# First stretch of the mixers: TensorE in an order of emission that follows a rough account of its time, windows of the projection reordered

## The chip, the cores and the metric

The kernel runs on one core of one Trainium2 chip. The metric is the time of one execution on the device in microseconds (us); what is compared is the median over runs. Matrix products run on TensorE (PE in the profile), elementwise work on VectorE (DVE), ScalarE (ACT) and GpSimd (POOL), and transfers are issued by SyncE (SP), ScalarE and GpSimd.

## The reference

A trunk of two layers over 512 prompt positions and 8 samples of 4 positions, 544 columns in all. A layer is a gated feed-forward part, four mixers side by side, and a second feed-forward part:

```python
def _layer(x, pos0, st, p):
    x = x + 0.5 * _swiglu(_rmsnorm(x, p['norm_ffn1']), p['ffn1_in'], p['ffn1_out'])
    u = _rmsnorm(x, p['norm_mix']) @ p['w_in']
    u_ssd, u_rwkv, u_s5, u_pool = _split_at(u, (SSD_PROJ, RWKV_PROJ, GROUP_WIDTH, GROUP_WIDTH))
    ...
    y = jnp.concatenate([y_ssd, y_rwkv, y_s5, y_pool], axis=-1)
    x = x + y @ p['w_out']
    x = x + 0.5 * _swiglu(_rmsnorm(x, p['norm_ffn2']), p['ffn2_in'], p['ffn2_out'])
```

The mixers that matter here take slices of the projected `u` (the normalized input times `w_in`):

```python
# rwkv: shifted inputs, low-rank decay and rate, then a scan over time
xs = uf + (prev - uf) * mu
w_raw = -softplus(-(w0 + tanh(wd) @ w2)) - 0.5
a = sigmoid(a0 + ad @ a2);  g = sigmoid(gd) @ g2
kk = k * k_k;  kk = kk / max(sqrt(sum(kk * kk)), 1e-12)
# s5: a complex linear recurrence, gelu, then a gated product
y = gelu(real(C h) + u * d_skip)
ya, yb = split(y @ glu_w + glu_b);  out = ya * sigmoid(yb)
# pool: running means over 2, 4, 8 and 16 positions, minus u, times pool_w
```

All is float32; a large product is made of two-part operands, so that a block costs three products of TensorE's faster float32 type.

## The kernel before, in words

The 544 columns lie along the free dimension in two halves; features lie on the 128 partitions. A layer's **mixers** begin with the projection. Its output is cut into 21 *windows* of 128 features (the last one, `dt`, of 8), each named for what it carries: `wa` (decay and rate inputs of rwkv), `k0 k1 r0 r1 v0 v1 gd` (rwkv), `s0 s1` (S5), `p0 p1` (pooling), `B C x z dt` (the SSD mixer). A window is eight blocks of weights with six matmuls each (`mm3`, L839 to L841) into one of two large PSUM buffers (`psd`), and is then multiplied by the reciprocal norm on VectorE into a tile `u` (the eviction, L1047 and L1050). The table `WIN` gives the windows' order. `UB` = 3 tiles `u` go round.

The *first stretch*, from `wa` to the products KB,AB (L220), runs two flows: `s5` and, one behind the other, `rwkv_prep` and `pool`. They are Python generators, and `merge` (L101) picks the one with the smallest account; a `yield` adds a fixed cost to it. When a flow asks for a window with `U(n)`, `win()` emits windows until that one is there. What the program emits, a scheduler then places on each engine's queue; on TensorE it moves instructions of the stretch past each other where operands allow. A *second stretch* follows (the chunks of rwkv, its samples, the SSD mixer, the remaining windows).

The steps that the prediction speaks of, by name and line:

- `wa` is shifted (L146 to L149), its upper half goes through tanh on ScalarE (L152), and four products `xs,mat` (through the helper `mm544`, L126; each is two matmuls of 272 columns) give `sig` and `av` (L159, L160).
- `sq` (L167) and its product (`sq,cst`) give `ss` (L169); `rsqrt` (L132 to L135) and L173 to L187 then make the operands RA, KB and `xs` on VectorE.
- `s5` takes each half `t` of its groups through DRAM into `U8` (L710 to L713), multiplies by GT (L721), rotates and scans on VectorE (L725 to L733), rotates back into `HP` (L740), and multiplies by TP and CO (L749, L750). The result goes through DRAM into `yg` (L753), gets the skip term (L755) and gelu (L756). The products `yg,glu` (L764) need both halves.
- `pool` makes running sums by adds on VectorE (L563), forms `pP` (L574 to L579) and multiplies it.
- Weights are split into a rounded part `whi` on ScalarE (L823) and the rest `wlo` (L826), which in the mixers is GpSimd's.

Of the kernel before, what the change touches and what calls it, by code (L numbers as in the profile page):

```python
# [100 lines left out]
def merge(*flows):  # L101

    q=[[t,i,f,g] for i,(t,f,g) in enumerate(flows)]
    while q:
        e=min(q,key=lambda e:(e[0],e[1]))
        try: e[0]+=e[2]*next(e[3])
        except StopIteration: q.remove(e)
class Mix:
    def __init__(s,tc,nc,ctx):
        s.tc,s.nc,s.ctx=tc,nc,ctx  # L110
# [11 lines left out]
    def mm544(s,lhsT,rhs,fn):  # L122

        for i in range(2):
            ps=s.bank()[:,:H]; c=slice(i*H,(i+1)*H)
            s.nc.tensor.matmul(ps,lhsT,rhs[:,c],start=True,stop=True)  # L126
# [10 lines left out]
    def rwkv_prep(s,U,fp,tp,R):  # L137

        nc=s.nc; V=nc.vector; A=nc.scalar; G=nc.gpsimd; PE=nc.tensor
        tmp=lambda n="tmp": tp.tile([128,T],F32,name=n,tag="tmp")  # L140
        def shift(n,x=None):
# [7 lines left out]
            V.scalar_tensor_tensor(xv,us[:,:,1:5],om,ts,op0=OP.mult,op1=OP.add)  # L149
            return x  # L150
        wa=shift('wa')
        A.activation(wa[0:64],wa[0:64],AF.Tanh)  # L152
        yield 4
# [3 lines left out]
        for p in range(2):  # L157
# [6 lines left out]
            yield 4  # L164
            ra=fp.tile([128,2,T],F32,name=f"RA{p}"); kb=fp.tile([128,2,T],F32,name=f"KB{p}"); RA.append(ra); KB.append(kb)
            xk=shift(f'k{p}')
            sq=tmp("sq"); A.activation(sq,xk,AF.Square,scale=s.v('kk',p))  # L167
            ss=tmp("ss")
            s.mm544(s.c('j64'),sq,lambda ps,c: V.tensor_scalar(ss[:,c],ps,1e-24,None,op0=OP.max))  # L169
            A.activation(sig,sig,AF.Exp,scale=-DC); Ex=sig  # L170
            yield 4
# [6 lines left out]
            yield 4  # L178
# [5 lines left out]
            yield 4  # L184
# [155 lines left out]
    def rwkv_sample(s,R,S0,state_out,sp):  # L340
        nc=s.nc; V=nc.vector; A=nc.scalar; G=nc.gpsimd; PE=nc.tensor
# [216 lines left out]
    def pool(s,U,emit,tp):  # L558
# [5 lines left out]
        for t in range(2):  # L564
            u=U(t); F=tl("pF"); a=tl("pA")
# [5 lines left out]
            yield 5  # L571
# [7 lines left out]
            V.tensor_tensor(P[:,0:16],m,u[:,15:31],op=OP.subtract)  # L579
# [211 lines left out]
class Kern(Mix):  # L791
# [218 lines left out]
    def mixers(s,l,st):  # L1010
# [255 lines left out]
```

## Time and profile before

| | |
|---|---|
| median of 3 runs | 2235.03 us (2230.42 to 2238.39) |
| the profiled execution | 2238.23 us, its span 2236.1 us |
| TensorE busy | 2148.0 us (96% of the span) |
| VectorE, ScalarE, GpSimd busy | 69%, 53%, 25% |
| first stretch of layer 0 | 399.56 to 536.69 us |
| first stretch of layer 1 | 1500.82 to 1641.41 us |

The profile is one execution. A timeline row is one instruction, or a run of like ones with their count, with its start and length; behind it, in brackets, stands how long the engine was idle before it and what ended that. A matmul of float32 operands is two records. [...]

### The profile page before, as it was taken

Reading aid. Unit: us, or ns where it says so; the run is one execution under the profiler, and the core shown is the slowest. Engines: PE = TensorE matmul, PEld = TensorE weight load, DVE = VectorE, ACT = ScalarE, POOL = GpSimd, SP = SyncE. Lnnn points to the kernel's source line nnn. Section 1 sums busy time; section 2 is a strip of 40 time slices with the busy share of each in tenths; the row PEclk is TensorE's granted clock in tenths of the full one; section 3 lists DMA queues with packets and bytes.
Section 4 is the critical chain, followed back from the end, with each engine's and each line's share of the span. In section 5 each row is a group of like instructions: output and inputs, shape, how many; then the busy total and the mean of one; then the engine's idle time right before and its main releaser. Section 6 shows DMA issues by size and latency. Waiting matters only on the chain. (4 is left out here: it accounts for less than half of the span.)

```text
span 2236.1 us, 42540 instructions
## 1 busy us (share of the span) xinstructions
PE 2148.0 (96%) x16630; PEld 2091.5 (94%) x16630; DVE 1550.0 (69%) x2895; ACT 1195.2 (53%) x2251; POOL 555.4 (25%) x650
## 2 busy tenths in 40 slices
PE   8999999989999999999999999998889999999997
PEld 8999999987799989999999999998878999999997
DVE  7877775288866887777577666644887678666664
ACT  6755554365444675555465555535553446555542
POOL 2111121534313411112141111123432124111112
PEclk9999999999999999999999999999899999999999
DMA  6666564542213466656357565554332135665551
GB/s 183 177 146 173 150 157 143 199 122 97 80 38 127 116 165 152 164 150 162 108 120 180 133 144 154 132 164 151 111 100 71 44 128 131 155 151 147 134 140 46
DMA packets 151560, 298.62 MB, mean 134 GB/s; under 512 B 37184, under 2 KB 61888, under 8 KB 151360
## 3 DMA queue, kind: packets, MB, share of 16 engines
q1 hardware_dynamic: 101600, 187.51, 25.4%
q0 software_dynamic: 35712, 65.55, 17.7%
q10 hardware_dynamic: 14048, 42.85, 5.8%
q8 instruction: 130, 2.13, 0.4%
q14 instruction: 70, 0.57, 0.1%
HBM read 202.10 MB, written 28.22 MB: 103 GB/s over the span
## 5 line engine op out<-in xcount | busy, mean ns | idle before, releaser
L938 PE MATMUL pm<-AH,xh 128*128 128x272 f32 x2016 | 527.0, 290 | 12.7 <-DVE e L942 6.0
L938 PE MATMUL pm<-AL,xh 128*128 128x272 f32 x2016 | 525.6, 289 | 0.0
L823 ACT CAST whi<-wraw 128x512 fp32r<-128x512 f32 x356 | 218.9, 617 | 360.2 <-PE pd L840 300.7
L839 PE MATMUL pd<-xh,whi 128*128 128x272 f32 (+2 forms) x1408 | 388.3, 295 | 14.0 <-DVE u L1050 5.1
L938 PEld LDWEIGHTS pm<-AH,xh 128*128 128x128 f32 x2016 | 380.6, 189 | 15.2 <-DVE e L942 7.6
L840 PE MATMUL pd<-xl,whi 128*128 128x272 f32 (+2 forms) x1408 | 392.6, 294 | 1.2 <-DVE xl L857 1.2
L938 PEld LDWEIGHTS pm<-AL,xh 128*128 128x128 f32 x2016 | 380.4, 189 | 0.0
L839 PE MATMUL pd<-hh,whi 128*128 128x272 f32 x1396 | 376.6, 289 | 0.0
L840 PE MATMUL pd<-hl,whi 128*128 128x272 f32 x1396 | 376.0, 288 | 0.0
L939 PE MATMUL pm<-AH,xl 128*128 128x272 f32 x2016 | 337.3, 289 | 1.8 <-DMA xl<-wraw 1.8
L825 POOL DMA_DIRECT2D xl<-wraw x144 | 124.9, 868 | 800.1 <-DVE s L942 584.3
L841 PE MATMUL pd<-xh,wlo 128*128 128x272 f32 (+2 forms) x1408 | 301.0, 293 | 1.2 <-DVE wlo L826 0.9
L939 PEld LDWEIGHTS pm<-AH,xl 128*128 128x128 f32 x2016 | 287.4, 189 | 2.1 <-DMA xl<-wraw 2.1
L841 PE MATMUL pd<-hh,wlo 128*128 128x272 f32 x1396 | 287.3, 287 | 0.0
L839 PEld LDWEIGHTS pd<-xh,whi 128*128 128x128 f32 x1408 | 269.2, 191 | 19.3 <-issue 12.4
L840 PEld LDWEIGHTS pd<-xl,whi 128*128 128x128 f32 x1408 | 270.0, 192 | 4.8 <-DVE xl L857 1.8
L839 PEld LDWEIGHTS pd<-hh,whi 128*128 128x128 f32 x1396 | 262.7, 188 | 1.7 <-issue 1.7
L840 PEld LDWEIGHTS pd<-hl,whi 128*128 128x128 f32 x1396 | 262.3, 188 | 0.0
L841 PEld LDWEIGHTS pd<-xh,wlo 128*128 128x128 f32 x1408 | 228.5, 191 | 3.4 <-DVE wlo L826 2.3
L841 PEld LDWEIGHTS pd<-hh,wlo 128*128 128x128 f32 x1396 | 219.6, 188 | 0.0
L826 DVE TENSOR_TENSOR wlo<-wraw,whi 128x512 fp32r<-128x512 f32 x256 | 184.6, 721 | 43.7 <-ACT whi L823 37.6
L970 DVE SCALAR_TENSOR_TENSOR x<-pd,x 128x544 f32<-128x544 f32 x159 | 114.7, 721 | 97.6 <-PE pd L841 97.1
(510 smaller groups left out, 3604.2 us busy)
## 6 DMA issues: line engine op xcount, KB each, us to landing
wraw<-in_w SPq DMA_DIRECT2D x262, 512.0 KB, 4.0
xl<-wraw POOLq DMA_DIRECT2D x144, 256.0 KB, 3.9
wraw<-in_w ACTq DMA_DIRECT2D x59, 512.0 KB, 3.4
xl<-sqa POOLq DMA_DIRECT2D x72, 256.0 KB, 3.4
AL<-ss POOLq DMA_DIRECT2D x16, 272.0 KB, 5.4
AL<-sqa POOLq DMA_DIRECT2D x16, 272.0 KB, 4.4
xd<-x SPq DMA_DIRECT2D x16, 272.0 KB, 2.9
x<-xd SPq DMA_DIRECT2D x16, 272.0 KB, 4.7
```

Source lines behind the costliest of these rows:

```text
L823: nc.scalar.copy(hi,x)
L825: nc.scalar.mul(lo,x,-1.0); nc.gpsimd.dma_start(lo,x,accum_op=OP.add)
L826: else: s.lo.tensor_tensor(lo,x,hi.bitcast(F32),op=OP.subtract)
L839: nc.tensor.matmul(p,wh,rh[:,a:b],start=(n==0),stop=False)
L840: nc.tensor.matmul(p,wh,rl[:,a:b],start=False,stop=False)
L841: for p,a,b in o: nc.tensor.matmul(p,wl,rh[:,a:b],start=False,stop=(n==K-1))
L938: for t in F[j]: nc.tensor.matmul(o,wh[:,j,:],t[:,f,:],start=first and j==0 and t is F[j][0],stop=False,skip_group_check=True)
L939: for j in range(4): nc.tensor.matmul(o,wl[:,j,:],F[j][0][:,f,:],start=False,stop=j==3,skip_group_check=True)
L970: V.scalar_tensor_tensor(xv,po[:,:,:H],0.5,xv,op0=OP.mult,op1=OP.add)
```

## The change

A class `Queue` stands before TensorE in the mixers and the projection. It adds up a rough time `t` of what is issued, and while `on` (the first stretch) it binds every instruction of a step to the last TensorE instruction of the step before (`issue_after`), so that TensorE runs them in the order of emission. `drive` takes the place of `merge`: a flow goes on when the window it named has been evicted and the delay that it yielded has passed on that account; otherwise `fill` emits half a window (four blocks). `room` holds a window back while three tiles `u` live.

```diff
+class Queue:
...
+    def run(s,f,us):
+        s.t+=us
+        if s.on and s.gate is not None:
+            with s.tc.issue_after(s.gate): i=f()
+        else: i=f()
+        s.last=i.ins
+    def matmul(s,o,lhs,rhs,**k):
+        n=math.prod(rhs.shape[1:])
+        s.run(lambda: s.e.matmul(o,lhs,rhs,**k),n*0.00046 if lhs.dtype==F32R else max(0.2,n*0.00172))
...
+    def drive(s,flows,fill,at):
+        q=[[0.0,None,g] for g in flows]
+        def adv(f):
+            a=s.t; s.gate=s.last; r=f(); at['now']+=s.t-a
+            for n in s.new: at[n]=at['now']
+            s.new.clear()
+            return r
+        while q:
+            for e in q:
+                if e[1] in at: e[0]=at[e[1]]; e[1]=None
+            e=next((e for e in q if e[1] is None and e[0]<=at['now']),None)
+            if e is not None:
+                y=adv(lambda: next(e[2],None))
+                if y is None: q.remove(e)
+                elif isinstance(y,str): e[1]=y
+                else: e[0]=at['now']+y
+            elif not adv(fill): at['now']=min(e[0] for e in q if e[1] is None)
```

In the flows the yields become names of windows and delays; in `s5` the tag `W` gets a third buffer and the staging of the second half is emitted after the first half's `HP`:

```diff
+        yield 'wa'
         wa=shift('wa')
         A.activation(wa[0:64],wa[0:64],AF.Tanh)
-        yield 4
+        yield 5.5
...
-            GT=v3(ld('GT',128,'W',2)); COS=v3(ld('COS',64,'COS',1)); SS=v3(ld('SS',64,'SS',1)); RHO=ld('RHO',64,'RHO',1)
+            GT=v3(ld('GT',128,'W',3)); COS=v3(ld('COS',64,'COS',1)); SS=v3(ld('SS',64,'SS',1)); RHO=ld('RHO',64,'RHO',1)
...
-            TP=v3(ld('TP',128,'W',2)); CO=v3(ld('CO',128,'W',2))
-            yield 6
+            TP=v3(ld('TP',128,'W',3)); CO=v3(ld('CO',128,'W',3))
+            t0=s.ev['now']+10
+            if t==0: yield from stage(1)
+            yield max(0,t0-s.ev['now'])
...
         nc.sync.dma_start(state_out['p'],hl); nc.sync.dma_start(state_out['s'],hs)
+        yield 13
```

The windows' order begins, before: wa k0 s0 r0 s1 v0 gd k1 p0 p1 v1 r1 B1; now: wa k0 s0 r0 v0 s1 k1 r1 v1 p0 gd p1 B1. The rest of the table stays. In `mixers`:

```diff
+        s.ev=at={'now':0.0}; s.live=set(); s.pe.on=True; s.pe.last=None; half=[]
+        def room(n):
+            if n in CONV_J: return len(s.live)+2<=UB
+            if n in SHIFT_J or n in ('dt','z0','z1'): return len(s.live)+1<=UB
+            return n!='p1' or 'p' not in s.live
+        def fill():
+            if half:
+                n,pd=half; half.clear()
+                for k in range(4,KD): s.mm3(pd,st[k],k,KD,COL)
+                evict(n,pd); return True
+            if not todo or not room(todo[0]): return False
+            n=todo.pop(0); pd=s.psd.tile([128,2,512],F32,name="pd")
+            if n=='dt': s.mmdt(pd,st,COL); evict(n,pd)
+            else:
+                for k in range(4): s.mm3(pd,st[k],k,KD,COL)
+                half.extend((n,pd))
+            return True
...
-            merge((*FL['s5'],s.s5(lambda t: get(f's{t}'),s.prep[l],io['mat'][l][:,1024:2048],io['s5h'][l],dict(p=io['s5_p'][l],s=io['s5_s'][l]),out(0),s.sc)),
-                  (*FL['prep'],seq(s.rwkv_prep(get,fp,tp,R),s.pool(lambda t: get(f'p{t}'),out(2),s.sc))))
+            s.pe.drive([s.rwkv_prep(get,fp,tp,R),s.pool(lambda t: get(f'p{t}'),out(2),s.sc),
+                s.s5(lambda t: get(f's{t}'),s.prep[l],io['mat'][l][:,1024:2048],io['s5h'][l],dict(p=io['s5_p'][l],s=io['s5_s'][l]),out(0),s.sc)],fill,at)
+            if half: fill()
+        s.pe.on=False; s.live.clear()
```

How instructions move is seen on the engines' queues. All matmuls through the new class carry its line L120, and the other lines are later by some 30 to 65.

**First group.** TensorE in layer 0, at the end of the window `k0` (`xh_5186` is its last operand) and the start of `s0` (`xh_4816`), before:

```order
L840 MATMUL pd<-xl_5187,whi 128x288
L841 MATMUL pd<-xh_5186,wlo 128x256
L841 MATMUL pd<-xh_5186,wlo 128x288
L839 MATMUL pd<-xh_4816,whi 128x256
L840 MATMUL pd<-xl_4817,whi 128x256
L839 MATMUL pd<-xh_4816,whi 128x288
```

and now:

```order
L120 MATMUL pd<-xl_5187,whi 128x288
L120 MATMUL pd<-xh_5186,wlo 128x256
L120 MATMUL pd<-xh_5186,wlo 128x288
L120 MATMUL pm<-xs,mat 128x272 x4
L120 MATMUL pd<-xh_4816,whi 128x256
L120 MATMUL pd<-xl_4817,whi 128x256
L120 MATMUL pd<-xh_4816,whi 128x288
```

The four products of `wa` now stand between the two windows; before, the windows `s0` to `v0` followed without them.

**Second group.** VectorE in layer 0, the S5 part's rotation of its second half, before (from its first copy to `HP`):

```order
L725 COPY sw<-X 64x512
L728 TENSOR_TENSOR xc<-X,pCOS 128x512
L729 TENSOR_TENSOR sw<-sw,pSS 128x512
L730 TENSOR_TENSOR xc<-xc,sw 128x512
L733 SCALAR_TENSOR_TENSOR gk<-pRHO,xc 128x512
L725 COPY sw<-gk 64x512
L739 TENSOR_TENSOR xc<-gk,pCOS 128x512
L738 TENSOR_TENSOR sw<-sw,pSS 128x512
L162 SCALAR_TENSOR_TENSOR cumS<-cst_5203,sig 128x544
L740 TENSOR_TENSOR HP<-xc,sw 128x8x63
```

and now (the stretch from L222 on; `HP` comes five rows behind the last one shown):

```order
L222 TENSOR_TENSOR RA_5788<-xs,cumS 128x544
L218 TENSOR_TENSOR xs<-xs,av 128x544
L769 COPY sw<-X 64x512
L219 TENSOR_TENSOR KB_5789<-xs,Ei 128x544
L772 TENSOR_TENSOR xc<-X,pCOS 128x512
L223 SCALAR_TENSOR_TENSOR xs<-xs,vec_72 128x544
L773 TENSOR_TENSOR sw<-sw,pSS 128x512
L1233 TENSOR_SCALAR om<-vec_73 128x2
L1234 TENSOR_SCALAR om<-vec_73 128x2
L774 TENSOR_TENSOR xc<-xc,sw 128x512
L777 SCALAR_TENSOR_TENSOR gk<-pRHO,xc 128x512
L1111 TENSOR_TENSOR u<-pd,rsq_r 128x512
```

TensorE now, where `HP` is wanted (the end of the window `p0`):

```order
L120 MATMUL pd<-xh_5186,wlo 128x256
L120 MATMUL pd<-xh_5186,wlo 128x288
L120 MATMUL pm<-U_5825,pTP 128x96
L120 MATMUL pm<-HP,pCO 128x96
L120 MATMUL pm<-U_5825,pTP 128x96
L120 MATMUL pm<-HP,pCO 128x96
```

The rotation stood almost alone before; now it is laced with the steps of `k1` and `r1` (L215 to L223), which begin eleven rows earlier with `ss`. On TensorE the products TP,CO of the second half stand behind `p0`.

**Third group.** VectorE in layer 0, the adds of the pooling of `p1` and the second `yg`, before:

```order
L1050 TENSOR_TENSOR u<-pd,rsq_r 128x8x4
L563 TENSOR_TENSOR pA<-pB 64x672
L1169 TENSOR_SCALAR om<-vec_73 128x2
L1170 TENSOR_SCALAR om<-vec_73 128x2
L563 TENSOR_TENSOR pF<-pA 64x664
L578 TENSOR_TENSOR pM<-pF,cst_5203 128x16
L1047 TENSOR_TENSOR u<-pd,rsq_r 128x512
L1050 TENSOR_TENSOR u<-pd,rsq_r 128x8x4
L755 SCALAR_TENSOR_TENSOR yg_6089<-u_s_5744,vec_72,yg_6089 128x576
```

and now:

```order
L602 TENSOR_TENSOR pA<-u_p 128x678
L602 TENSOR_TENSOR pB<-pA 128x676
L602 TENSOR_TENSOR pF<-pB 64x672
L602 TENSOR_TENSOR pA<-pB 64x672
L602 TENSOR_TENSOR pF<-pA 64x664
L613 SCALAR_TENSOR_TENSOR pP<-pF,cst_5203,u_p 128x512
L615 SCALAR_TENSOR_TENSOR pP<-pF,cst_5203,u_p 128x32
L799 SCALAR_TENSOR_TENSOR yg_6264<-u_s_5818,vec_72,yg_6264 128x576
```

TensorE now, at the end of the window `p1` (`xh_5186` again) and the start of `B1`:

```order
L120 MATMUL pd<-xh_5186,wlo 128x256
L120 MATMUL pd<-xh_5186,wlo 128x288
L120 MATMUL pm<-xs,mat 128x272 x4
L120 MATMUL pm<-yg_5864,glu 128x288 x2
L120 MATMUL pm<-yg_6264,glu 128x288 x2
L120 MATMUL pd<-xh_4816,whi 128x256
```

The second `yg` multiply stood behind the adds and ahead of the forms before; now it stands behind two of the forms. On TensorE only the four products of `g` lie between `p1` and the first products that need both `yg`; before, the windows `v1`, `r1` and most of `B1` lay between `p1` and those of the second `yg`.

## Rows read from the trace of the kernel before

**Rows 1.** TensorE by stretches of both layers: stretch; length, busy (count), PEclk, DMA share, GB/s.

```profile
399.56:536.69 137.13, 124.09 (x892) 0.98 0.45 145
1500.82:1641.41 140.59, 125.71 (x892) 0.95 0.45 144
```

**Rows 2.** Timeline of TensorE: start, length, instruction, count, wait and its releaser.

```profile
414.69 0.35 PE L839 MATMUL pd<-xh,whi 128*128 128x256 f32 x1 [2.10 <-DVE u L1050]
...
464.37 1.35 PE L721 MATMUL pm<-U,pGT 128*128 128x96 f32 x5 [4.96 <-DMA pRHO<-s5d]
...
482.39 0.73 PE L126 MATMUL pm<-sq,cst 128*128 128x272 f32 x2 [2.61 <-ACT sq L167]
...
511.68 0.75 PE L764 MATMUL pm<-yg,glu 128*128 128x288 f32 x2 [1.54 <-ACT yg L756]
...
1516.80 0.35 PE L839 MATMUL pd<-xh,whi 128*128 128x256 f32 x1 [2.96 <-DVE u L1050]
...
1566.21 1.35 PE L721 MATMUL pm<-U,pGT 128*128 128x96 f32 x5 [4.62 <-DMA yd<-Y]
...
1584.48 0.82 PE L126 MATMUL pm<-sq,cst 128*128 128x272 f32 x1 [4.21 <-ACT sq L167]
```

**Rows 3.** TensorE by stretches after four of these waits.

```profile
464.40:471.50 7.10, 7.10 (x26) 0.53 0.62 183
1516.80:1530.00 13.20, 13.20 (x106) 1.00 0.52 178
1566.20:1573.00 6.80, 6.79 (x34) 0.70 0.67 200
1584.50:1591.00 6.50, 6.50 (x27) 0.52 0.08 30
```

**Rows 4.** Timeline of ScalarE behind the eviction of `wa`, both layers.

```profile
417.24 0.66 ACT L152 ACTIVATE xs<-xs 64x544 f32<-64x544 f32 x1
...
1519.35 0.66 ACT L152 ACTIVATE xs<-xs 64x544 f32<-64x544 f32 x1
```

**Rows 5.** Timelines of VectorE and ScalarE: steps of `ss`, root and rotation.

```profile
451.01 1.22 DVE L733 TENSOR_TENSOR_SCAN gk<-pRHO,xc 128x512 f32<-128x512 f32 x1
...
453.90 0.78 DVE L169 TENSOR_SCALAR ss<-pm 128x272 f32<-128x272 f32 x2
...
454.60 0.68 DVE L738 TENSOR_TENSOR sw<-sw,pSS 128x512 f32<-128x512 f32 x1
...
454.76 1.28 ACT L132 ACT_TABLE_LOAD   x1 [1.83 <-DVE ss L169]
...
456.06 0.66 ACT L132 ACTIVATE rsq_r<-ss 128x544 f32<-128x544 f32 x1
...
461.38 0.72 DVE L180 TENSOR_TENSOR KB<-rsq_r,Ei 128x544 f32<-128x544 f32 x1
```

**Rows 6.** Timeline of TensorE: GT, the product of `sq`, what follows it.

```profile
442.02 1.92 PE L721 MATMUL pm<-U,pGT 128*128 128x96 f32 x16
...
452.12 1.08 PE L126 MATMUL pm<-sq,cst 128*128 128x272 f32 x4
...
453.03 0.58 PE L749 MATMUL pm<-U,pTP 128*128 128x96 f32 x4
```

**Rows 7.** Timelines of VectorE, ScalarE and GpSimd: pooling, `yg`, gelu, `wlo`.

```profile
482.29 0.86 DVE L563 TENSOR_TENSOR pF<-u_p 64x678 f32<-64x678 f32 x1
...
484.06 0.82 DVE L755 SCALAR_TENSOR_TENSOR yg<-u_s,vec,yg 128x576 f32<-128x576 f32 x1
...
497.61 1.95 DVE L563 TENSOR_TENSOR pA<-u_p 128x678 f32<-128x678 f32 x1
...
510.94 0.68 ACT L756 ACTIVATE yg<-yg 128x576 f32<-128x576 f32 x1
...
497.34 1.50 POOL L826 TENSOR_TENSOR wlo<-wraw,whi 128x512 fp32r<-128x512 f32 x1
```

**Rows 8.** Timeline of TensorE in layer 0's second stretch.

```profile
569.98 0.38 PE L363 MATMUL pm<-vu,L 64*64 64x64 f32 x2 [3.21 <-DVE vu L361]
```

More of the change, by code (lines that the diff above doesn't have):

```diff
@@ L125, in mm544 @@
             ps=s.bank()[:,:H]; c=slice(i*H,(i+1)*H)
[L126 removed]
+            s.pe.matmul(ps,lhsT,rhs[:,c],start=True,stop=True)
             fn(ps,c)
@@ L705, in s5, with stage @@
         G.tensor_tensor(hs,hs,ht,op=AD)
-        ge=[]
-        for t in range(2):
-            g8=slice(t*8,t*8+8)
+        ge=[]; staged={}
+        def stage(t):
+            yield f's{t}'
             us=U(t)
@@ L711, in s5 @@
             U8=tl("U8",[8,96],bufs=2); G.memset(U8[:,:,80:96],0.0)
-            yield 3
             for si in range(8): nc.sync.dma_start(U8[si*16:si*16+16,:,0:80],ud[t][:,:,si,:].rearrange("g c k -> c g k"))
+            staged[t]=us,U8,s.ev['now']+9.5
+        for t in range(2):
+            g8=slice(t*8,t*8+8)
+            if t==0: yield from stage(0)
+            us,U8,t0=staged[t]
             def ld(n,w,tag,bufs):
@@ L848, in mmdt @@
             for i,(a,b) in enumerate(cols):
-                for j in range(2): nc.tensor.matmul(ps[0:8,i,0:b-a],wh[:,0:8],st[n][j][:,a:b],start=(n==0 and j==0),stop=(n==KD-1 and j==1))
+                for j in range(2): s.pe.matmul(ps[0:8,i,0:b-a],wh[:,0:8],st[n][j][:,a:b],start=(n==0 and j==0),stop=(n==KD-1 and j==1))
     def split(s,k,x,scale=None,pool=False):
@@ L1028, in mixers, with evict @@
         CONV_O=[xs[0],xs[1],BB[:,0,:],BB[:,1,:],CCt[:,0,:],CCt[:,1,:]]
-        U={}; SD={}; dtg=[]; todo=list(WIN)
+        U={}; SD={}; dtg=[]; todo=[n for n,_ in WIN]
         rs=None; s.lo=G
         COL=[(0,256),(256,T)]
+        s.ev=at={'now':0.0}; s.live=set(); s.pe.on=True; s.pe.last=None; half=[]
[15 more added lines that the diff above has]
+            return True
         def win():
+            for g in dtg: next(g,None)
+            while len(U)<len(WIN) and (fill(),half)[1]: pass
+        def evict(n,pd):
             nonlocal rs
-            for g in dtg: next(g,None)
-            n,_=todo.pop(0)
-            M=8 if n=='dt' else 128
-            pd=s.psd.tile([128,2,512],F32,name="pd")
-            if n=='dt': s.mmdt(pd,st,COL)
-            else:
-                for k in range(KD): s.mm3(pd,st[k],k,KD,COL)
+            s.pe.new.append(n); M=8 if n=='dt' else 128
             if rs is None: rs=s.rstd(st['acc'],up,tp,'tmp')
+            if s.pe.on:
+                if n in SHIFT_J or n in ('dt','z0','z1'): s.live.add(n)
+                elif n in ('p0','p1'): s.live.add('p')
             r2=rs[0:M,0:NP].rearrange("p (a b) -> p a b",a=2); pp=pd[0:M,:,0:256]
```

67 lines of the change are left out of this document (36 added, 31 removed).

## Prediction

> **What bounds the kernel now.** I read the profile from the coarse to the fine. The share of busy time on the page (TensorE 96%, in the table above) says that TensorE is the bound nearly everywhere, so the time changes only where TensorE idles or runs at its lower clock. The table by stretches then gives the part that the change reorders: in layer 0 the first stretch of the mixers lasts 137.13 us, of which TensorE is busy 124.09, and in layer 1 it lasts 140.59 with 125.71 busy [rows 1]. The idle time is 13.04 and 14.88 us, and that is all that a better order could remove, apart from the clock. The timeline of TensorE names the waits [rows 2]: in layer 0 there are 2.10 for the first eviction (`u`), 4.96 for a load that the staged S5 product needs (`RHO`), 2.61 for `sq` and 1.54 for the gelu `yg`; in layer 1 the first three are 2.96, 4.62 and 4.21. These make 11.21 and 11.79, so small waits are the other 1.8 and 3.1.
>
> Last the clock. In the 7.1 us after the wait of 4.96 the granted clock is 0.53, after that of 4.62 it is 0.70 over 6.8 us, after that of 4.21 it is 0.52 over 6.5 us, while after the wait of 2.96 it is 1.00 [rows 3]. [...] **Before, the two stretches therefore lose** 13.0 + 3.3 = 16.3 us and 14.9 + 2.0 + 3.1 = 20.0 us. The amount of TensorE work is the same before and after, so I only have to set the losses of the new order against these.
>
> **The change, part by part.** TensorE's instructions of the first stretch now stand in the order of emission, so whatever waits at the head stops all windows behind it. I walked that order with the durations of the old trace. What goes: the `RHO` wait (the third `W` buffer and the earlier staging put the S5 loads well ahead) and the `sq` wait (the window `r0` or `r1` now covers it). Five things cost, or could.
>
> (a) *The first lora product.* After the projection `k0` the four products `xs,mat` now stand ahead of `s0` (the first group of order rows). Before, `s0` needed only the first eviction. The products need `tanh` of `wa`: TensorE is out of work at 414.69 - 2.10 = 412.59 [rows 2], the `tanh` starts at 417.24, behind its table load, and ends at 417.90 [rows 4]. ScalarE's order up to there is unchanged, so this wait is 5.3, with its signal 5.4, where 2.10 was. In layer 1 work ends at 1516.80 - 2.96 = 1513.84 and the `tanh` at 1519.35 + 0.66 = 1520.01: 6.2 where 2.96 was. Nothing covers it, since `s0`, `r0` and `v0` stand behind. I am surest of this term.
>
> (b) *TP/CO of the second S5 half.* They need `HP`, and VectorE now has, between `ss` of `k1` and `HP`, the whole `k1`/`r1` block with the rotation of the S5 half laid between (the second group of order rows). From the start of `sq`'s pair of products: the pair 1.08, the second half of `ss` 0.4, then the load of the root's table, which waited for `ss` in the old trace, 1.28, root and square 0.66 each, signals 0.1 = 4.2 us [rows 5]. Then 19 operations of 512 or 544 columns at 0.68 to 0.72, say 0.70, 13.3, the scan 1.22 [rows 5], and four pairs of small or half-width ones, 2.0 by an estimate from their widths: 16.5. `HP` is there 20.7 after. TensorE meanwhile has the pair, which makes room for the next product after 0.91, the eight GT products, 1.92 [rows 6], and the windows `v1` and `p0`. A window is 48 matmuls, and 106 took 13.2 [rows 3], so 6.0 each. That is 0.91 + 1.92 + 12.0 = 14.8. Wait: 20.7 - 14.8 = 5.9, in each layer. From below it is 3, if the 19 overlap so that each costs 0.55; from above 8, if two are as long as the longest of [rows 7].
>
> (c) *The gated product of the S5 part.* Its first four matmuls need both `yg`. The second `yg` on VectorE now stands behind the whole pooling of `p1`, and TensorE has only the four products of `g` to do after `p1` (the third group of order rows). From `p1`'s last matmul: eviction 0.8, five adds of 0.86 = 4.3, two forms of 0.75 and 0.25 less their overlap = 0.9, `yg` 0.82, gelu 0.68 = 7.5 [rows 7] (eviction and forms are estimates from operations of their width). Four products are two pairs at 0.91 [rows 6], 1.8. Wait: 7.5 - 1.8 = 5.7 where 1.54 was. It can't be under 3, since the adds alone are 4.3, and reaches 7.9 with two long adds.
>
> [...] An add took 1.95 instead of 0.86 at 497.61, and GpSimd's `wlo` subtraction had started 0.27 before it and ended at 498.84 [rows 7]: 498.84 + 0.86 = 499.70, close to its end at 499.56. [...] In the sum I take the undisturbed durations, since most operations of [rows 5] and three of the five adds had them; the other case is rival C.
>
> (d) *Small waits* stay at layer 0's 1.8 in both layers. The 12 more table loads lie on ScalarE, 53% busy, and none stands on the chains of (a) to (c) beyond the loads counted there: 12 x 1.28 = 15 us that I cost at nothing, hidden beside TensorE's windows; two on the path would be 2.6.
>
> (e) *The second stretch* has fewer W_out products to fill its end, and its sample chain changes places with the `tc` blocks: the longest wait there is 3.21 for `vu` [rows 8]. I cost it at 0, between -3.2 - 2.8 = -6 per layer, if that wait and its clock loss go, and +4, an estimate of little more than that wait over again, if `vu` queues behind the block.
>
> **The sum.** The three new waits, 5.4 to 6.2, are longer than those that were followed by the lower clock, so each brings 2.8. Layer 0: 5.4 + 5.9 + 5.7 + 1.8 + 3 x 2.8 = 27.2 against 16.3, +10.9. Layer 1: 6.2 + 5.9 + 5.7 + 1.8 + 8.4 = 28.0 against 20.0, +8.0. Together +18.9. By the profiled execution that is 2238.2 + 18.9 = 2257.1; this execution lies 3.2 above the median of the runs shown, 2235.0, so I forecast 2253.9, say **2254 us, slower by 0.8%**. What a measurement of this kernel can tell from no change is 0.3%, 6.7 us.
>
> **Rivals.**
>
> *A, faster.* VectorE keeps up. It is decided at one place, (b): whether the queue of VectorE from `ss` on gives `HP` within 14.8 us instead of 20.7, before TensorE is through with `p0`. Without that backlog (c) goes to its lower end, 3, and a wait of 3 wasn't followed by the lower clock [rows 3]. Layer 0 then loses 5.4 + 2.8 + 3 + 1.8 = 13.0 (-3.3) and layer 1 13.8 (-6.2): 2235.0 - 9.5 = 2225.5. For it: the old waits for `RHO` and `sq` are surely gone, 4.96 and 2.61 [rows 2]. Against it: none of the nineteen operations can be passed, and at 0.70 each they alone are 13.3. Chance 0.23.
>
> *B, the clock holds.* If the new waits aren't followed by half clock, as that of 2.96 wasn't [rows 3], 6 x 2.8 = 16.8 goes: 2237, no change. Much the same comes out if just one of (b) and (c) is covered in both layers, 2 x (5.7 + 2.8) = 17.0. Against it: the three waits over 4 us were. Chance 0.12.
>
> *C, GpSimd in the way.* Two of the operations in (b) and two in (c) as long as the one of 1.95: 4 x 1.09 = 4.4 per layer, 2253.9 + 8.7 = 2263. Chance 0.10.
>
> *D, no effect.* The gate sets an order in which TensorE would be held by evictions and PSUM banks just as before: 2235. The order rows show different neighbours at each wait, so 0.03.
>
> **Chances.** Forecast 0.52; with C slower by over 0.3% is 0.62; B and D make 0.15 within; A 0.23 faster. The range, 2218 to 2266, holds A with some of what (e) may give back, and C with a little of what (e) may add; below it lies about 0.11, where (e) gives back most of its 12 as well, above it 0.06.
>
> **What would show it.** Right: in the new trace, waits of 5 to 6 us ahead of the first `xs,mat`, of the second TP/CO and of the first `yg` product in both layers, each followed by a granted clock near 0.5, and no wait ahead of GT. Wrong: the second TP/CO or the `yg` product starting without a wait, or the first stretch from `wa` to the first KB,AB shorter than 137 and 141 us.

## The result, and the profile after

The changed kernel takes **2270.6 us** (median of 4 runs, 2267.1 to 2271.5) where the kernel before took 2236.7 beside it: the ratio is 1.0143, with a 95% interval of 1.0125 to 1.0162. So it is slower, by 1.4%. The direction was forecast; the size was not, and the time lies 4.6 us above the range. The profiled execution took 2271.07 us with a span of 2269.3, which is 33.2 more than before.

The page says what kind of time that is: TensorE was busy 2148.0 us before and is busy 2155.4 now, 7.4 more. The rest of the span, in which it stands still, went from 88.1 to 113.9, 25.8 more. Three quarters of the loss is idle time; the work has stayed the same (16630 matmuls on both pages), so the other 7.4 us are the same products taking longer.

The windows of TensorE over the first stretch of both layers (from `wa` to the first KB,AB), then over the second (to the end of the mixers), columns as in [rows 1] (PEclk is the granted clock of TensorE as a share of its full one):

```profile
399.54:548.13 148.59, 126.76 (x876) 0.92 0.43 134
1518.87:1667.67 148.80, 126.96 (x876) 0.92 0.43 136
548.13:755.53 207.40, 191.95 (x1474) 0.99 0.27 80
1667.67:1876.31 208.64, 191.81 (x1475) 0.99 0.27 79
```

The second stretch of the kernel before, in the same view:

```profile
536.69:737.02 200.33, 188.76 (x1460) 0.98 0.27 82
1641.41:1843.46 202.05, 191.26 (x1459) 0.97 0.27 81
```

The idle time of the first stretch went from 13.04 to 148.59 - 126.76 = 21.83 us and from 14.88 to 21.84 [rows 1], +15.8 together. That of the second went from 11.57 to 15.45 and from 10.79 to 16.83, +9.9. Together +25.7: all of the added idle time lies in the mixers, and 9.9 of it where the prediction had set nothing. (A part of each stretch's length is only a shift: some 16 matmuls now stand behind the first KB,AB, as the counts show.)

TensorE's waits over 3 us in the first stretch, which answer to [rows 2]:

```profile
418.22 0.82 PE L120 MATMUL pm<-xs,mat 128*128 128x272 f32 x1 [5.65 <-ACT xs L188]
...
453.43 0.82 PE L120 MATMUL pm<-xs,mat 128*128 128x272 f32 x1 [3.49 <-ACT bo L228]
...
494.53 0.75 PE L120 MATMUL pm<-HP,pCO 128*128 128x96 f32 x2 [5.68 <-DVE HP L783]
...
523.41 1.33 PE L120 MATMUL pm<-yg,glu 128*128 128x288 f32 x2 [5.76 <-ACT yg L800]
...
1537.69 0.82 PE L120 MATMUL pm<-xs,mat 128*128 128x272 f32 x1 [5.79 <-ACT xs L188]
...
1613.97 0.74 PE L120 MATMUL pm<-HP,pCO 128*128 128x96 f32 x2 [5.56 <-DVE HP L783]
```

The waits for `RHO` and for `sq` are gone, as foretold, and the three new ones stand at the three places named: 5.65, 5.68 and 5.76 in layer 0 (layer 1: 5.79, 5.56 and 5.76). A fourth, of 3.49 in both layers, was not foretold. Behind all four the granted clock is low, 0.50 to 0.60 in layer 0. The windows there, as in [rows 3]:

```profile
418.22:422.30 4.08, 4.08 (x10) 0.52 0.77 234
453.43:457.00 3.57, 3.57 (x16) 0.60 0.31 79
494.53:501.00 6.47, 6.47 (x31) 0.53 0.43 138
523.41:528.00 4.59, 4.59 (x16) 0.50 0.00 0
```

Time at a granted share c is counted here as lost by 1 - c, an estimate: behind the wait of 3.49 the same four matmuls of a window took 0.93 us at 0.50 (454.93 to 455.86) and 0.51 at 1.00 (457.04 to 457.55). That is 4.08 x 0.48 + 3.57 x 0.40 + 6.47 x 0.47 + 4.59 x 0.50 = 8.7 us; layer 1, by the same four windows, gives 8.8. So the first stretch loses 21.83 + 8.72 = 30.6 and 21.84 + 8.78 = 30.6 us, where 27.2 and 28.0 were forecast.

In the second stretch the longest wait is now one for a load, 2.37 us in layer 0 and, in layer 1:

```profile
1709.46 1.22 PE L120 MATMUL pm<-S,as 128*128 128x512 f32 x1 [3.65 <-DMA S<-in_rw]
```

Before, no wait of TensorE over 0.8 us in this stretch was for that load, and the longest was the 3.21 for `vu` [rows 8], which is down to 1.26.

**The fourth wait** is a queue behind a queue. The two products of `bo` fill two PSUM banks of the few that all small products take in turn, and ScalarE copies them out (L228). TensorE's next `xs,mat` needs the second bank. In ScalarE's timeline the copy that frees it stands behind the S5 part's copy `sw<-gk`:

```profile
452.48 0.62 ACT L769 COPY sw<-gk 64x512 f32<-64x512 f32 x1 [3.32 <-DVE gk L777]
453.00 0.37 ACT L228 COPY bo<-pm 128x272 f32<-128x272 f32 x1
```

and that one waits for VectorE's scan, in VectorE's timeline:

```profile
449.55 1.64 DVE L774 TENSOR_TENSOR xc<-xc,sw 128x512 f32<-128x512 f32 x1
451.22 1.23 DVE L777 TENSOR_TENSOR_SCAN gk<-pRHO,xc 128x512 f32<-128x512 f32 x1
```

ScalarE stood still for 3.32 us, although both products of `bo` had been done at 447.72 (they begin at 446.54 and take 1.18). The copy `bo` starts only behind `sw<-gk`, at 453.00 against 452.48. With TensorE bound to its order as well, one blocked copy on ScalarE stopped all products behind it, for 3.49 us.

### The profile page after: what moved, and what is told of

Read it like the earlier page. It is cut to its first block, busy times and chain, and to the rows that moved or that the text cites. A ratio compares the mean times of both kernels' runs of the same rounds, so it can differ in the third digit from the quotient of the medians.

```text
span 2269.3 us, 42554 instructions
## 1 busy us (share of the span) xinstructions
PE 2155.4 (95%) x16630; PEld 2092.1 (92%) x16630; DVE 1538.6 (68%) x2895; ACT 1211.4 (53%) x2263; POOL 552.3 (24%) x650
## 3 DMA queue, kind: packets, MB, share of 16 engines
q0 software_dynamic: 35712, 65.55, 17.4%
## 4 chain that ended last, share of the span: by engine, by line
PE 76%; DVE 12%; ACT 4%; issue 3%; DMA 3%; POOL 1%; ACTq 0%; SPq 0%; DVEq 0%; POOLq 0%
PE pd L120 35%; PE pm L983 21%; PE pm L984 11%; PE pm L120 8%; DVE u L452 1%; DVE wlo L871 1%; DVE sq L928 1%; PE pm L121 1%; POOL wlo L871 1%; DVE TL L278 0%; DVE tmL L277 0%; ACT whi L868 0%; DMA x<-in_x 0%; DVE rsq_q L167 0%; DVE AL L871 0%
## 5 line engine op out<-in xcount | busy, mean ns | idle before, releaser
L120 PE MATMUL pd<-xh,whi 128*128 128x272 f32 (+3 forms) x1440 | 399.3, 297 | 10.4 <-DVE gt L966 4.3
L120 PE MATMUL pd<-xl,whi 128*128 128x272 f32 (+3 forms) x1440 | 397.3, 292 | 3.7 <-POOL xl L900 1.9
L120 PE MATMUL pd<-hh,whi 128*128 128x272 f32 x1396 | 376.7, 289 | 0.0
L120 PE MATMUL pd<-hl,whi 128*128 128x272 f32 x1396 | 376.1, 288 | 0.0
L120 PE MATMUL pd<-xh,wlo 128*128 128x272 f32 (+2 forms) x1408 | 295.1, 291 | 1.9 <-DVE wlo L871 1.6
L120 PEld LDWEIGHTS pd<-xh,whi 128*128 128x128 f32 (+1 forms) x1440 | 272.1, 189 | 17.9 <-issue 5.8
L120 PE MATMUL pd<-hh,wlo 128*128 128x272 f32 x1396 | 287.3, 287 | 0.0
L120 PEld LDWEIGHTS pd<-xl,whi 128*128 128x128 f32 (+1 forms) x1440 | 272.5, 189 | 8.8 <-DVE xl L902 2.8
L120 PEld LDWEIGHTS pd<-hh,whi 128*128 128x128 f32 x1396 | 262.7, 188 | 1.7 <-issue 1.7
L120 PEld LDWEIGHTS pd<-hl,whi 128*128 128x128 f32 x1396 | 262.3, 188 | 0.0
L120 PEld LDWEIGHTS pd<-xh,wlo 128*128 128x128 f32 x1408 | 226.7, 190 | 4.4 <-DVE wlo L871 3.3
L120 PEld LDWEIGHTS pd<-hh,wlo 128*128 128x128 f32 x1396 | 219.5, 188 | 0.0
L871 POOL TENSOR_TENSOR wlo<-wraw,whi 128x512 fp32r<-128x512 f32 x100 | 137.2, 1375 | 187.8 <-ACT whi L868 159.5
```

The lines of the kernel that those rows point to most:

```text
L120: s.run(lambda: s.e.matmul(o,lhs,rhs,**k),n*0.00046 if lhs.dtype==F32R else max(0.2,n*0.00172))
L871: else: s.lo.tensor_tensor(lo,x,hi.bitcast(F32),op=OP.subtract)
```

## The experiments

The theory after the result: each late product costs its wait and the clock behind it, and each can be put right by moving it later in the order. The rival: the stretch follows one chain through VectorE and ScalarE, and a product put later only finds the next late one. All ratios are against the kernel before in the same job; the changed kernel's own is 1.0143.

### Delaying one late product at a time

*e3_wa* gives the products of `wa` room for the tanh.

```diff
-        yield 5.5
+        yield 8.5
```

> Changed kernel with the delay behind tanh of wa 8.5 instead of 5.5, so that half of the window s0 stands ahead of the first four products xs,mat. Theory (each new wait is a price of its own: its idle time and the half clock after it, and goes with its cause): the wait of 5.65 and 5.79 us goes back to some 2.1 and 2.9 for the first eviction, which the clock didn't answer before; that gives back 3.6 + 1.9 in layer 0 and 2.9 + 2.0 in layer 1, 10.4 us: about 2260 us. Rival (the stretch is as long as VectorE's queue, so a wait removed comes back at the next wait): 2267 to 2272, with a longer wait ahead of the products of bo or of TP/CO.

Measured: 1.0131 (1.0115 to 1.0147), no gain. The wait for the tanh is gone (2.21 for the eviction `u` is left), but TensorE's timeline has these two in its place, where there was no wait and 5.68:

```profile
436.25 0.99 PE L120 MATMUL pm<-U,pGT 128*128 128x96 f32 x7 [2.38 <-DMA U<-ud]
...
496.30 0.74 PE L120 MATMUL pm<-HP,pCO 128*128 128x96 f32 x2 [8.81 <-DVE HP L783]
```

and VectorE's timeline just ahead of `HP`, with operations that took 0.72, 0.43 and 0.74 in the changed kernel:

```profile
483.73 1.80 DVE L218 TENSOR_TENSOR xs<-xs,av 128x544 f32<-128x544 f32 x1
485.56 1.40 DVE L769 COPY sw<-X 64x512 f32<-64x512 f32 x1
...
493.90 1.75 DVE L181 SCALAR_TENSOR_TENSOR xv<-u,om,sh 128x512 f32<-128x512 f32 x1
```

Counted from the start of the stretch, TensorE came 1.2 us earlier to the pair of `sq` (472.25 - 399.16 = 73.1 instead of 74.3), and `HP` ended 2.2 us later (97.1 instead of 94.9). What was taken out ahead came back at `HP`, and more. But not by the order of VectorE's queue alone: each of the three operations ran beside a `wlo` subtraction of GpSimd (483.11 to 486.68 and 493.71 to 495.10). Four operations took longer so, by 4.1 us, where it was two in the changed kernel, by 2.1; that is 2 of the 3.4 us by which the way from the pair of `sq` to the end of `HP` grew (23.99 instead of 20.64).

*e4_hp* delays the second TP,CO, *e5_glu* the `yg` products, *e6_bo* the next products behind `bo`.

```diff
# e4_hp
-            t0=s.ev['now']+10
+            t0=s.ev['now']+(10 if t==0 else 13)
# e5_glu
-        yield 13
+        yield 16
# e6_bo
             nc.sync.dma_start(sp[p],bo)
+            if p==0: yield 2
```

> Changed kernel with the delay ahead of the second TP/CO 13 instead of 10, so that half of the window gd and the products of bo stand ahead of it; the products of yg move back by half a window with it. Theory of single prices: the wait for HP goes from 5.6 to some 1.9 without half clock, 3.8 + 3.1 per layer, and that for yg from 5.76 to 2.8, 3.0 + 2.3 per layer: 24 us in all, 2246. Rival (VectorE's queue sets the length): the wait for HP shrinks but that for yg grows or stays, 2258 or more.

> Changed kernel with the delay ahead of the products of yg 16 instead of 13: half of the window B1 stands ahead of them. Theory of single prices: the wait of 5.76 becomes 2.8 and isn't followed by half clock: 2 x (3.0 + 2.3) = 10.6 less, 2260. Rival: the wait comes back ahead of KB,AB or in the second stretch, 2267 to 2272.

> Changed kernel with a step of half a window (the second half of s1) between the products of bo of the first half of rwkv and the four products xs,mat of the second. Theory: the wait of 0.57 + 3.49 us that the prediction didn't have comes from the PSUM banks: the second copy of bo on ScalarE stands behind a copy that waits for VectorE's scan, and the products need its bank; with half a window between, it is gone with its half clock: 2 x (4.1 + 1.4) = 11 less, 2260. Rival (the products wait for something else, or the time comes back at HP): 2267 to 2272.

Measured: 1.0202 (1.0173 to 1.0231), 1.0192 (1.0174 to 1.0209) and 1.0164 (1.0149 to 1.018). The first two are slower than the changed kernel; the third is by its median, 2278.0, while the intervals still overlap. In e4_hp the wait for `HP` has become one for an eviction, and waits that were not there stand in the second stretch:

```profile
493.94 0.55 PE L120 MATMUL pd<-xh,whi 128*128 128x256 f32 x1 [5.36 <-DVE u L1114]
...
612.08 0.39 PE L120 MATMUL pd<-xh,whi 128*128 128x272 f32 x1 [3.22 <-ACT xh L900]
...
660.94 1.29 PE L120 MATMUL pm<-t,N 128*128 128x128 f32 x5 [3.65 <-DVE t L293]
```

The first shows why delaying didn't help: the window put ahead needs an eviction from the same VectorE that is behind with `HP`. The second stretch, with the other two waits in it, lasts 213.5 and 213.7 us instead of 207.4 and 208.6. With the delays the account reaches the first KB,AB later, so that they stand behind the whole window `C0` and the chunks' chain starts later beside its cover; that this is what opens the two waits is likely, and not shown. In e5_glu the `yg` wait only went from 5.76 to 3.87, with the same two new waits of 3.22 and 3.65. In e6_bo the `bo` wait shrank from 3.49 to 1.37, and these took its place:

```profile
458.26 0.74 PE L120 MATMUL pm<-U,pTP 128*128 128x96 f32 x2 [3.44 <-ACT sig L195]
...
501.06 0.74 PE L120 MATMUL pm<-HP,pCO 128*128 128x96 f32 x2 [8.80 <-DVE HP L784]
```

So the theory of single prices falls as a forecast of the time: four delays, no gain. The times of e5_glu and e6_bo lie above its rival's 2267 to 2272 too, and the rival's single chain isn't shown by these runs. In e4_hp and e5_glu the first stretch holds 26 or 27 matmuls more (3.3 or 3.4 us, at 6.0 for 48) and yet lasted 147.79 and 150.78 us, and 149.60 and 150.87, so at equal work it got shorter by 1 to 4 us; what was gained there was lost in the second stretch, and more.

### Undoing one half of the change

*e1_nogate* keeps all but the binding; *e2_oldwin* keeps the binding and takes the old order of windows.

```diff
# e1_nogate
-        if s.on and s.gate is not None:
+        if False:
# e2_oldwin: the line WIN of the kernel before
```

> Changed kernel with the binding of TensorE's instructions to the step before switched off; flows, delays and the order of windows stay, and the scheduler may again place TensorE's instructions past each other (it then puts 46 of 48 matmuls of s0 ahead of the first products xs,mat, but leaves TP/CO behind p0 and the products of yg behind p1). Theory (the held order is what puts the late products ahead of ready windows): only the wait for tanh and that for bo go, 2 x (3.4 + 1.9) + 2 x (4.1 + 1.4) = 22 at most, about 2250, and the waits for HP and yg stay. Rival (the order of the windows and the order on VectorE that follows from it cost the time, the binding nothing): the waits come back as longer ones at HP and yg, 2265 to 2275.

> Changed kernel with the windows in the order of before (s1 and gd early, v1 and r1 late), the queue, its binding and the delays kept. If the held order is the cause, the time stays near 2270 or is worse, 2262 to 2285, with waits ahead of xs,mat, HP and yg as long as now. If the new order of the windows is the cause, it comes back to before, 2236 to 2250.

Measured: 1.0072 (1.0053 to 1.0091), a median of 2255.8 us, and 1.0188 (1.0167 to 1.0209). The binding alone is worth half of the loss, 0.7%, some 15 us. Without it the first stretch lasts 140.02 and 139.59 us, near the 137.13 and 140.59 of before [rows 1], and the second stays long, with 15.4 and 16.9 us idle:

```profile
399.16:539.18 140.02, 123.79 (x878) 0.96 0.45 142
...
539.18:750.22 211.04, 195.60 (x1473) 0.97 0.26 79
1652.31:1862.16 209.85, 192.96 (x1474) 0.98 0.27 79
```

The expectation was half missed: the waits for `HP` and `yg` didn't stay but fell, in layer 0 to 0.62 and 0.96, and a wait for a weight cast came in both layers. It returns below:

```profile
479.13 0.58 PE L120 MATMUL pd<-xh,whi 128*128 128x256 f32 x1 [5.38 <-ACT whi L868]
```

The old order of windows under the binding is worse than the new one. The wait for `HP` is gone there, and one of 5.38 for the pooling's `pP` has come; those for the tanh (5.21) and `yg` (4.54, all in layer 0) stay.

The same two halves were put into the kernel before: *e11_w3* only the three buffers `W`, *e12_winonly* only the new line `WIN`.

```diff
# e11_w3, in ld('GT',..), ld('TP',..) and ld('CO',..)
-...128,'W',2)
+...128,'W',3)
# e12_winonly: the line WIN of the changed kernel
```

> Kernel before with one part of the change alone: three W buffers for the S5 loads instead of two. The wait of 4.96 and 4.62 us ahead of the second GT products comes, by this reading, from the GT load, which has to wait until the first TP products have given a buffer back; with a third buffer it goes, with the half clock behind it: 2 x 4.8 + 3.3 + 2.0 = 15 less than before, ratio 0.993 (2222 against 2237). Rival (what is removed comes back at sq, HP or yg, as in the kernels with the held order): ratio 0.997 to 1.002.

> Kernel before with the windows in the order of the change alone; merge, yields, buffers and the scheduler's freedom as before. If the order of windows costs what the unbound changed kernel still lost (some 17 us), the ratio is 1.006 to 1.010. If it is harmless and that rest comes from the delays and the staging, the ratio is 0.997 to 1.003.

Measured: 0.9993 (0.998 to 1.0006) and 1.0026 (1.0013 to 1.0039). The buffers take the wait ahead of the second GT products away and gain nothing. So that wait, which the trace puts down to the load `RHO`, was one for the load of GT, whose buffer is one of `W`: that load is now issued at 453.47 instead of 460.35, while `RHO`'s is issued only at 461.44, behind the start of the GT products at 460.67. With GT done, TensorE now waits exactly as long at the next products, 68 us into the stretch, for VectorE:

```profile
467.55 1.70 PE L126 MATMUL pm<-xs,cst 128*128 128x272 f32 x3 [4.96 <-DVE xs L187]
```

In the kernel before these products stood behind GT, and VectorE finished their operand at 466.15:

```profile
465.38 0.77 DVE L187 SCALAR_TENSOR_TENSOR xs<-xs,vec 128x544 f32<-128x544 f32 x1
```

TensorE was out of work from 464.37 - 4.96 = 459.41. Had GT (1.92) stood ready there, it would have been done at 461.33 and TensorE idle for the 4.8 us up to 466.15. So the 4.96 us of [rows 2] that the change set out from were never there to be had. The new order of windows alone costs 0.26%, some 6 us, less than the 0.6 to 1.0% that would have explained what the unbound kernel still loses.

### Moving work between the stretches

*e8_yg* exchanges the windows `p1` and `B1` and sends the stores of `g` through ScalarE's queue; *e9_gt* brings the second GT forward, so that the rotation stands ahead of the `k1` block on VectorE.

```diff
# e8_yg
-...('p1',2436),('B1',640)...
+...('B1',640),('p1',2436)...
-            nc.sync.dma_start(sp[2+p],g)
+            nc.scalar.dma_start(sp[2+p],g)
# e9_gt
-            staged[t]=us,U8,s.ev['now']+9.5
+            staged[t]=us,U8,s.ev['now']+(9.5 if t==0 else 6.5)
```

> Changed kernel with the windows p1 and B1 exchanged and the store of g issued by ScalarE, so that the second yg stands ahead of the pooling of p1 on VectorE and its load no longer behind the store of g on SyncE. Theory: the wait of 5.76 ahead of the first products of yg and the half clock behind it go in both layers, 2 x (5.8 + 2.3) = 16: about 2254. Rival (the end of the stretch waits for the chains whatever stands at this place): it comes back ahead of KB,AB or in the second stretch, 2265 to 2272.

> Changed kernel with the delay between the staging of the second S5 half and its GT products 6.5 instead of 9.5, which puts GT half a window earlier on TensorE, ahead of the product of sq, and so the rotation and HP ahead of ss and the k1 block on VectorE; TP/CO then stands behind half of p0, and the second yg ahead of the pooling of p1. Theory (the waits for HP and yg come from VectorE's order alone): both go, 2 x (5.6 + 3.1) + 2 x (5.8 + 2.3) = 33.6 less, 2237 if nothing takes their place; those for tanh and bo stay as they are. Rival (the stretch is as long as its chain through VectorE, whatever its order): the k1 block is late instead, and the time comes back ahead of the products of bo, of g or KB,AB: 2258 or more.

Measured: 1.0105 (1.0085 to 1.0126) and 1.0107 (1.0085 to 1.0129), both some 8 us better than the changed kernel. In e9_gt the wait for `HP` is gone, and `yg` waits longer:

```profile
514.87 1.81 PE L120 MATMUL pm<-yg,glu 128*128 128x288 f32 x3 [8.11 <-ACT yg L800]
```

The wait for the load `S` of the second stretch grew as well, to 4.28 and 4.25, and the first stretch has 20.23 and 22.43 us of idle time where it was 21.83 and 21.84: nearly all of the wait came back as others, as the rival had it. Where the 8 us lie instead isn't traced.

In e8_yg the `yg` wait only fell to 4.47, but the second stretch fell to 201.1 and 201.3 us. Which of its two edits does that was left open, and *e17_gst* (the store alone) and *e18_swap* (the exchange alone) tell them apart.

> The changed kernel with one edit: the two stores of g go out on ScalarE's queue instead of SyncE's. It is one half of the run e8_yg (2262.65, 8 under the changed kernel). Theory (SyncE's queue: the stores of g hold the loads of the second stretch, where TensorE waits 2.37 and 3.65 for S out of in_rw): those waits go, the second stretch is 3 to 5 us shorter per layer and the time is 2261 to 2265. Rival (the gain is the exchange of the windows p1 and B1, which puts more TensorE work between yg's adds and the chunks): the second stretch keeps its 207 and 208 us and the time is 2268 to 2273.

> The other half: the windows p1 and B1 exchanged in the order, the stores of g left on SyncE's queue. TensorE's order is that of the run e8_yg, instruction for instruction. Theory (SyncE's queue): 2268 to 2273, with the wait for S out of in_rw above 2 in both layers. Rival (the exchange): the wait for yg 4.5, the second stretch near 201 us, the time 2261 to 2265.

Measured: 1.0149 (1.0132 to 1.0166) and 1.0121 (1.0098 to 1.0144). In medians the store alone is where the changed kernel is (2270.1), and the exchange alone is where both together are (2262.8). The intervals of the ratios alone would not part them, the windows of the second stretch do. Store alone:

```profile
546.70:754.85 208.15, 191.95 (x1474) 0.99 0.27 80
1666.15:1876.87 210.72, 194.21 (x1475) 0.98 0.26 79
```

and exchange alone:

```profile
552.82:753.60 200.78, 188.43 (x1445) 0.98 0.28 82
1669.10:1869.70 200.60, 187.34 (x1445) 0.99 0.27 81
```

The theory of SyncE's queue falls. Some 29 matmuls went back ahead of the first KB,AB with the exchange, which only shifts time, but the idle time of the second stretch also fell, from 15.45 and 16.83 to 12.35 and 13.26, near the 11.57 and 10.79 of before. So a part of what the second stretch lost hangs on which window ends the first. The wait for the load `S` goes with it, to under 0.8 in layer 0 and to 1.04 in layer 1; why the chunks' chain goes better behind `p1` than behind `B1` stays open.

### VectorE or ScalarE behind it

*e13_free* joins the two edits that gained: no binding, and those of e8_yg.

> Changed kernel without the binding and with p1 and B1 exchanged and the store of g on ScalarE. The two alone gave 15 and 8 us back. If they act at different places (the binding in the first stretch, the exchange in the second), both add up: 2270 - 23 = 2248. If they give the same time back, 2253 to 2258.

Measured: 1.0032 (1.0017 to 1.0047), 2245.9 us where 2248 was expected if the gains add up. What is left is close to the 0.26% that the order of windows cost by itself in e12_winonly, where `p1` still stood ahead of `B1`; the delays and the staging, which no run took out, can then cost little here. The largest wait of that kernel, in both layers, was 5.38 us for a weight cast on ScalarE (first TensorE's row, then ScalarE's):

```profile
478.43 0.58 PE L120 MATMUL pd<-xh,whi 128*128 128x256 f32 x1 [5.38 <-ACT whi L868]
```

```profile
477.46 0.40 ACT L767 COPY X<-pm 128x320 f32<-128x320 f32 x1
477.76 0.61 ACT L868 CAST whi<-wraw 128x512 fp32r<-128x512 f32 x1
```

The cast stands behind the copy `X`, and that behind the block of roots and exponentials. *e14_xv* moves the copies `X` to VectorE in this kernel, *e15_xvb* does so in that of e8_yg, where TensorE's order is bound and stays the same:

```diff
-                A.copy(X[:,g0:g0+4,:],pv[:,:,0:80])
+                V.tensor_copy(X[:,g0:g0+4,:],pv[:,:,0:80])
```

> The kernel of the run e13_free (binding off, p1 and B1 exchanged, store of g on ScalarE's queue) with the two copies X out of PSUM on VectorE instead of ScalarE, nothing else. In that run TensorE waited 5.38 in both layers for a weight cast that stood on ScalarE behind the second copy X, with about 4 us at half clock behind it. Theory (what is left over the kernel before is ScalarE's queue, where a weight cast stands behind the k1 block): the wait of 5.38 goes, each layer gains 5.4 to 9, and 2245.9 becomes 2228 to 2235, level with the kernel before or under it. Rival (VectorE is the chain that bounds the stretch, so four more copies of 0.4 on it come out at HP and yg): the cast's wait goes, but waits for HP and yg of over 2 us come in, and the time stays at 2243 to 2250.

> The same move of the copies X to VectorE with the binding on, beside the run e8_yg (2262.65; TensorE's order is the same as there, instruction for instruction). Theory (in the bound order the waits at HP and yg are set by VectorE's chain, which ScalarE's queue does not touch): the waits 5.6 for HP and 4.5 for yg stay within 0.8 and the time is 2258 to 2266. Rival (part of those waits is ScalarE's queue, through the copies into the rotation, the casts and the copy of bo): the waits for HP or bo shrink by over 2 in each layer and the time is 2245 to 2255.

Measured: 1.0077 (1.0062 to 1.0092), so 0.45% or 10 us slower than e13_free, and 1.0118 (1.0095 to 1.014), which the intervals don't part from e8_yg. The cast's wait went, from 5.38 to 1.27, and one for VectorE took its place:

```profile
478.98 0.39 PE L120 MATMUL pd<-xh,whi 128*128 128x256 f32 x1 [1.27 <-ACT whi L868]
...
500.24 0.74 PE L120 MATMUL pm<-HP,pCO 128*128 128x96 f32 x2 [3.42 <-DVE HP L783]
```

Four copies of 0.5 us on VectorE cost 5 us per layer, and freeing ScalarE gained nothing. That is the rival's outcome, and past its 2250: without the binding it points to VectorE's chain as what the stretch hangs on; why 2 us of copies cost 5 isn't shown. With the binding the evidence is weaker: `HP` waited 4.36 and 5.84 there where it had been 5.68 and 5.56, `yg` 4.47 as in e8_yg, and the time, 2267.4, lies above both ranges. VectorE's windows in the changed kernel, over the whole first stretch and from the pair of `sq` to `HP`, show how the share of the page (68%) can hide that:

```profile
399.54:548.13 148.59, 83.11 (x140) 0.92 0.43 134
473.83:494.47 20.64, 18.54 (x33) 0.98 0.21 59
```

56% busy over the stretch, 90% in the 20.64 us that decide.

No version tried beats the kernel before; e11_w3 ties with it.

## Why the prediction was right or wrong

**(a) The first lora product: right.** 5.65 and 5.79, forecast 5.4 and 6.2. In layer 0 the chain on ScalarE ran 0.27 us later than in [rows 4].

**(b) HP: right in its size, and by errors that cancel, which is luck.** From the pair of `sq` at 473.83 to the end of `HP` at 494.47 it took 20.64 us, forecast 20.7. But the chain's head was 0.9 shorter: the root's table was loaded before `ss` began, where I had taken the load to wait for `ss` as in [rows 5] (first ScalarE's row, then VectorE's):

```profile
474.41 1.28 ACT L165 ACT_TABLE_LOAD   x1
```

```profile
474.80 0.78 DVE L206 TENSOR_SCALAR ss<-pm 128x272 f32<-128x272 f32 x2
```

Two operations were nearly as long as rival C had it, each while GpSimd subtracted a `wlo`: 1.70 and 1.87, together 2.1 more than in e3_wa, where they took 0.72 and 0.78 with no `wlo` beside them. The other operations, begun before the ones ahead had ended, made the rest of the chain 1.2 shorter (L222 starts at 482.86 and L218 at 483.49, 0.63 apart): 17.4 in all from 477.09 to the end of `HP`, 15.3 without those two excesses, forecast 16.5. VectorE's timeline:

```profile
484.70 1.70 DVE L219 TENSOR_TENSOR KB<-xs,Ei 128x544 f32<-128x544 f32 x1
...
486.92 1.87 DVE L223 SCALAR_TENSOR_TENSOR xs<-xs,vec 128x544 f32<-128x544 f32 x1
```

and GpSimd's:

```profile
484.35 1.46 POOL L871 TENSOR_TENSOR wlo<-wraw,whi 128x512 fp32r<-128x512 f32 x1
486.93 1.29 POOL L871 TENSOR_TENSOR wlo<-wraw,whi 128x512 fp32r<-128x512 f32 x1 [1.11 <-ACT whi L868]
```

The first subtraction ends at 485.81; 0.7 more is 486.51, and KB ends at 486.40: like the add of [rows 7], it ends about its usual length behind the subtraction that began ahead of it. (For the second pair the starts lie 0.01 apart, too close to say which came first.) What holds the operation up isn't shown. I had weighed the longer operations, as rival C, and left them out of the sum.

**(c) yg: right, again by errors that cancel.** 5.76, forecast 5.7. The first add took 1.53 instead of 0.86, again beside a `wlo` of GpSimd (515.39 to 516.66), and the chain 8.5 instead of 7.5, from the end of `p1`'s last matmul at 514.85 to the gelu's end at 523.35; but TensorE had 2.8 us to do, not 1.8, because the first two of the four products need only the first `yg`, which I had misread.

**(d) Small waits: wrong.** "Small waits stay at layer 0's 1.8 in both layers." They are 21.83 - 17.09 = 4.74 and 4.73, for the wait of 3.49, with 1.4 to 1.5 of clock behind it that I hadn't counted. I had followed TensorE's order against VectorE's, but not the PSUM bank that a product needs and ScalarE's queue, in which the copy that frees it stands. That is 2.9 + 1.4 us per layer, less 1.1 because the three other waits cost 7.3 of clock and not 8.4. No run shows the 2.8 that the sum adds for each wait as a fixed price: it is the mean of 3.3, 2.0 and 3.1, estimates from the shares of [rows 3] (7.1 x 0.47, 6.8 x 0.30 and 6.5 x 0.48), and behind the three foretold waits of layer 0 the changed kernel showed 2.0, 3.0 and 2.3 in its place, by the same estimate.

**(e) The second stretch: wrong**, and the largest miss. "I cost it at 0." Both stretches together are 355.99 - 337.46 = 18.5 and 357.44 - 342.64 = 14.8 us longer, of which the first stretch's losses explain 14.2 and 10.6. The other 4.3 and 4.2 us are the upper end that the text had named, but for other reasons. The second stretch has 3.9 and 6.0 us more of idle time, and about 2 and 4 us less at the lower clock (0.99 instead of 0.98 and 0.97, two digits that leave 1 us open), so some 2 per layer net. The other 2 stand in rows that count as busy, and I haven't traced them to a place. The idle time isn't the wait for `vu`, which shrank, but that for the load `S` (2.37 and 3.65) and several of 0.8 to 1.4 us, and the exchange of two windows showed that part of it hangs on how the first stretch ends.

In sum: first stretch 30.6 + 30.6 - 36.3 = 24.9 instead of 18.9, and the 8.5 us of (e) make 33.4, about the 33.2 between the spans. Since (e) is what the stretches' lengths leave over, this shows only that the whole loss lies in the two stretches, not that (e) is explained.

**The rivals.** A (VectorE keeps up) falls: `HP` came after 20.64 and not 14.8. B (the clock holds) falls: all eight waits of 3.49 us or more in the first stretches were followed by 0.50 to 0.64. C was right in part: three operations beside a `wlo` took longer (1.70, 1.87 and 1.53 us) instead of four, but they didn't add to the time, being met by the savings named in (b) and (c). D falls. The decision that failed was the range: I let (e) reach +4 per layer and (d) not at all, and then left both together outside it.

## What to carry to other kernels

An order held on one engine turned every late operand into a stop for all that was queued behind (half of the loss here, 0.7 of 1.4%), so each of them has to be checked, and also the engine that empties the buffer into which the product goes. Before the price of a wait is booked as a gain, look at what the products behind it wait for: 4.96 us for a load became 4.96 us for VectorE at the next product. And a share of busy time over a stretch (56%) says nothing of the 20 us in it that decide (90%); to delay the product that waits there did not help in e4_hp, where what was put ahead of it needed the same engine.

## What the runs showed of the hardware that was not expected

The granted clock behind waits of 2.2 to 2.5 us goes either way. In e1_nogate it held in the 4 us behind a wait of 2.47 and fell behind one of 2.43:

```profile
414.67:418.67 4.00, 4.00 (x32) 1.00 0.48 147
...
446.64:450.64 4.00, 4.00 (x21) 0.61 0.87 245
```

and in e3_wa it fell behind a wait of 2.21 (0.57 over the next 4.00 us) and held behind one of 2.38 (1.00). So the price of 2.8 us per wait can't be tied to the length of the wait alone in that region. And the load of an activation table need not wait for the operand of the function behind it: the same load waited 1.83 us for `ss` in [rows 5] and started 0.4 us ahead of `ss` in the changed kernel, right behind the cast ahead of it (473.78 + 0.62 = 474.40). What makes the difference isn't shown.
